# One encoder layer on one core: value loads a step ahead, w_out's maxima in the projections' sweep, its split by halves, MLP seam's loads regrouped

## Chip, core and metric

The kernel runs on one core of a Trainium2 chip as one program. The metric is the device time of one launch in microseconds (us); of several runs the median is given. Engines: PE multiplies matrices (PEld loads its weights), DVE, ACT and POOL work on vectors, SP issues nearly all of the transfers (DMA). PE writes to PSUM banks; everything else lies in SBUF tiles of 128 partitions.

## What is computed

One layer of a bidirectional encoder on x (2048 tokens, 1024 wide, float32):

```python
h = rmsnorm(x); proj = h @ w_in          # c_q | c_kv | k_rope | dq | dk | dv
# A: latent attention, 4 heads: q, k (128 + 64 rotary, normed), v from c_q, c_kv
o_mla  = softmax(q @ k.T * 192**-0.5) @ v
# B: differential attention, 4 heads of 2 maps, with a bias by distance
o_diff = (softmax(s1) - lam * softmax(s2)) @ dv     # each head RMS-normed
x = x + concat(o_mla, o_diff) @ w_out
x = x + relu(rmsnorm(x) @ w_up)**2 @ w_down
```

## The kernel before

Nearly every product is made from two float16 (or fp32r) halves of a float32 operand: `split` (L129 without a scale, L130 with one) writes the high half h on ACT and the low half l = x - h on DVE, and `mm3` (L134 to L136) multiplies hh, hl and lh. A weight or value tile in float32 ("raw") is so loaded, scaled by a factor that comes from a maximum, and split before PE can use it. Tiles come from rotating pools: L (7 buffers), W (22), P (8), X4 (3) and N2 (6); a new tile waits until some buffer of its pool has been read to its end. A scheduler sets each engine's order from the program's order and a simulated timeline; chains of `ordered` instructions keep theirs, and `behind` sets a point ahead of which an instruction may not go.

**The stages.** *Projections' sweep*: sixteen iterations of about 26 us, one token tile each. `load_x` (L371, pool X4) loads x two tiles ahead, `make_xT` (L385) transposes it on PE, `sweepA_mid` writes the transposed low-rank projection cT (also X4), and queries, keys and values go to DRAM (qA, qB, kA, kB, kR, vD).

*Attention*: 64 steps, 4 heads x 16 query tiles. A step handles one query tile of one head, in both attentions: three softmaxes, 0 for the latent attention and 1 and 2 for the two maps of the differential one. Its order is written out in PROG as tokens: S scores on PE (L735), M maxima on DVE (L745, L750), N the shift nm of the exponentials (L755, L756), E exponentials on ACT (L762), diff (L805), hi (L813 on ACT for d = 1, L140 on POOL for d = 0) and lo (L819, POOL) the two halves of the probabilities, T their transposing transfer (L824, SP), pv the product with the values (L836 to L838), store (L842, then a transfer to oD). A mark ' means the step before, '' (written ") the one before that. `load0` and `load1` are where the program may do a piece of other work. In heads 0 to 2 load0 prepares the next head: in odd steps a transposing key load (L588), and in steps VQ = (2, 6, 10, 15) a load of a block of values (L601, 512 KB, pool P) with its split (L130) directly behind it in the program. In head 3 load0 is `wo_step`: steps 0 to 7 load a block of w_out (L884), steps 1 to 8 take the maximum of the block before (`wo_stat`, L900, DVE), step 8 has `wo_front` (L907 to L911 with L889), step 9 `wo_scale` (a matmul and a maximum across partitions, L895 to L897, and L913 to L917); from step 9 on the same blocks are loaded a second time, and each is split by the next step. The last two splits stand at the start of `out_proj`.

*out_proj and the seam*: x + mix @ w_out for the sixteen tiles, its RMS norm and transposes (`out_back`, L1085, L1088). `combine_rows` (L1056 ff.) forms seven combinations of token halves (a Strassen scheme of 7 products for 2 x 2 blocks) and `put` splits them (L129): for the first half of the columns (c = 0) into hT[0], for the second into DRAM as hcD, from where they are loaded again as hT[1]. `up_load` loads raw w_up, `up_stat` (L1168 ACT, L1171 DVE) and `up_scale` (L1178 to L1184) find its scale, `up_weights` splits it.

*MLP up*: 32 steps (p, c), a pair of column blocks of w_up by a half of the tokens. A step's seven products go to three banks X, Y, Z; the first is evicted by ACT (L1300) into the half u11 of a tile `ca` (pool X4), others into `cb` (pool P) and, at the end, u21 of `ca` (L1312, L1316, L1321, L1322 on DVE, L1306, L1309, L1327, L1328 on ACT). `up_rest` then combines ca and cb on POOL (L1350 to L1359), splits the results (L1346 ACT, L1347 DVE) and stores them to uD. *MLP down* follows and is not touched.

## Time and profile before

| | us |
|---|---|
| median of 3 runs | 2865.11 (2864.14 to 2866.52) |
| the profiled execution | 2862.0 |
| its span | 2860.2 |
| PE / DVE / ACT / POOL busy in it | 2686.4 / 2140.0 / 1735.5 / 1715.3 |
| projections' sweep until | about 455 |
| attention | 455 to 1405 |
| out_proj | 1405 to 1621 |
| MLP up | 1621 to 2250 |
| MLP down | 2250 to 2860 |

A timeline row reads: start, duration, engine, line, operation, tile written <- tiles read, shape, and in brackets how long the engine had idled and what ended it. A row of a group gives busy time, mean ns of one, idle time ahead and its releaser. A wait is put down to the event that came last. A row of a stretch ends with PE's granted clock (1.00 is full), the busy share of the DMA engines, and GB/s.

### The profile page before, as it was taken

How to read it: one execution, taken by the hardware profiler on the slowest of the kernel's cores; microseconds unless marked ns; L12 is line 12 of the kernel's file. 1: busy time of each engine (PE TensorE's matmuls, PEld its weight loads, DVE VectorE, ACT ScalarE, POOL GpSimd, SP SyncE). 2: the span in 40 equal slices, each digit the busy share in tenths (PEclk: the TensorE clock that was granted, in tenths of full speed). 3: DMA queues.
4: the chain of work that ended last, by engine and by line, in shares of the span. 5: the costliest groups of instructions: out<-in, count | busy, mean ns of one | idle time of the engine just before them, and what ended most of it. 6: DMA issues, size and time to landing. Idle time of an engine off the chain costs nothing. (4 is left out here: it accounts for less than half of the span.)

```text
span 2860.2 us, 47994 instructions
## 1 busy us (share of the span) xinstructions
PE 2686.4 (94%) x16904; PEld 1574.4 (55%) x16904; DVE 2140.0 (75%) x4292; ACT 1735.5 (61%) x3814; POOL 1715.3 (60%) x1404
## 2 busy tenths in 40 slices
PE   7999998999999999889899988999999899999999
PEld 6878885666656666556555434444444344444444
DVE  8767778999998999889868777777776655555543
ACT  6545556888888888778757656666666433333332
POOL 5434334888888888778724355444444755565544
PEclk9999999999999999999999999999999999999999
DMA  5445557998999999899844753444444643333334
GB/s 194 123 116 133 136 131 186 199 204 184 203 207 200 195 203 204 189 197 188 207 165 146 241 175 107 133 133 133 133 146 158 234 151 133 133 123 116 133 103 169
DMA packets 994514, 469.35 MB, mean 164 GB/s; under 512 B 776128, under 2 KB 943040, under 8 KB 994272
## 3 DMA queue, kind: packets, MB, share of 16 engines
q1 hardware_dynamic: 994272, 466.29, 62.7%
q8 instruction: 132, 2.16, 0.3%
q14 instruction: 110, 0.90, 0.1%
HBM read 168.39 MB, written 132.12 MB: 105 GB/s over the span
## 5 line engine op out<-in xcount | busy, mean ns | idle before, releaser
L762 ACT ACTIVATE P<-D,nm,one 128x512 f32<-128x512 f32 x768 | 587.2, 774 | 132.0 <-DVE nm L756 70.8
L735 PE MATMUL D<-W,X 128*128 128x512 f16 x2304 | 573.0, 384 | 61.6 <-ACT P L762 58.7
L819 POOL TENSOR_TENSOR L<-P,L 128x1024 f16<-128x1024 f32 x256 | 553.9, 2172 | 32.4 <-ACT L L813 21.8
L750 DVE TENSOR_REDUCE nmx<-D 128x1 f32<-128x512 f32 (+3 forms) x768 | 450.8, 619 | 38.3 <-PE D L735 32.1
L836 PE MATMUL O<-W,L 128*128 128x128 f16 x2048 | 363.0, 220 | 16.3 <-DMA L<-L 9.1
L1459 POOL TENSOR_TENSOR W<-W,N 128x512 f32<-128x512 f32 x192 | 242.6, 1273 | 222.6 <-DVE W L1457 220.0
L735 PEld LDWEIGHTS <-X 128*128 128x128 f16 x2304 | 214.2, 99 | 282.7 <-issue 94.3
L837 PE MATMUL O<-W,L 128*128 128x128 f16 x2048 | 362.8, 220 | 1.1 <-DVE W L130 1.1
L838 PE MATMUL O<-W,L 128*128 128x128 f16 x2048 | 363.0, 220 | 0.0
L1457 DVE SCALAR_TENSOR_TENSOR W<-D,dsc,W 128x512 f32<-128x512 f32 x224 | 166.3, 747 | 255.8 <-PE D L136 255.8
L134 PE MATMUL D<-W,W 128*128 128x512 f16 (+2 forms) x822 | 313.6, 382 | 24.1 <-ACT P L1309 11.4
L135 PE MATMUL D<-W,W 128*128 128x512 f16 (+2 forms) x822 | 313.3, 381 | 3.2 <-DVE W L130 3.2
L136 PE MATMUL D<-W,W 128*128 128x512 f16 (+2 forms) x822 | 312.9, 381 | 0.6 <-DVE W L130 0.5
L140 POOL TENSOR_SCALAR L<-P 128x1024 f16<-128x1024 f32 x128 | 223.1, 1743 | 138.7 <-ACT P L762 138.7
L134 PE MATMUL D<-L,W 128*128 128x512 f16 (+1 forms) x644 | 249.5, 387 | 18.0 <-ACT X L1300 12.1
L134 PE MATMUL D<-L,P 128*128 128x512 f16 x648 | 247.1, 381 | 14.5 <-ACT N L1453 14.2
L135 PE MATMUL D<-L,W 128*128 128x512 f16 (+1 forms) x644 | 247.4, 384 | 0.0
L136 PE MATMUL D<-L,W 128*128 128x512 f16 (+1 forms) x644 | 247.3, 384 | 0.0
L135 PE MATMUL D<-L,P 128*128 128x512 f16 x648 | 246.9, 381 | 0.0
L136 PE MATMUL D<-L,P 128*128 128x512 f16 x648 | 246.8, 381 | 0.0
L836 PEld LDWEIGHTS <-L 128*128 128x128 f16 x2048 | 201.2, 98 | 53.0 <-DMA L<-L 15.7
L837 PEld LDWEIGHTS <-L 128*128 128x128 f16 x2048 | 201.2, 98 | 46.2 <-issue 12.8
(421 smaller groups left out, 5729.5 us busy)
## 6 DMA issues: line engine op xcount, KB each, us to landing
P<-uD SPq DMA_DIRECT2D x124, 448.0 KB, 4.9
uD<-P SPq DMA_DIRECT2D x96, 512.0 KB, 3.2
P<-in_w_up_dram SPq DMA_DIRECT2D x34, 512.0 KB, 4.7
W<-in_w_down_dram SPq DMA_DIRECT2D x32, 512.0 KB, 4.1
X<-in_x_dram SPq DMA_DIRECT2D x17, 512.0 KB, 3.6
vD<-N SPq DMA_DIRECT2D x32, 256.0 KB, 2.6
qA<-N SPq DMA_DIRECT2D x32, 256.0 KB, 2.6
oD<-N SPq DMA_DIRECT2D x128, 64.0 KB, 2.6
```

Source lines behind the costliest of these rows:

```text
L134: mm(o, ah, bh, start=first, stop=False, skip_group_check=more),
L135: mm(o, ah, bl, start=False, stop=False, skip_group_check=more),
L136: mm(o, al, bh, start=False, stop=last, skip_group_check=more),
L140: return G.tensor_scalar(o, i, sc, 0.0, ALU.mult, ALU.add)
L735: ordered(mm(s, st, mv[:, kc], start=j == 0, stop=j == len(self.passes) - 1))
L750: ordered(V.tensor_reduce(self.nmx[:, self.n : self.n + 1], s[:, c0 * P : c1 * P], AX, ALU.max))
L762: last_exp[:] = [act(o, self.ch[c], AF.Exp, bias=self.nm, scale=self.sg, accum_out=self.sm[:, c : c + 1])]
L819: ordered(G.tensor_tensor(hl[:, 1], self.soft[d].p[hf], hl[:, 0], ALU.subtract))
L836: ordered(mm(od, hT_, v[:, 0], start=kb == 0, stop=False))
L837: ordered(mm(od, hT_, v[:, 1], start=False, stop=False))
L838: ordered(mm(od, lT_, v[:, 0], start=False, stop=kb == NT - 1))
L1459: G.tensor_tensor(x, x, part.pop((t, to)), ALU.add)
```

## The change

**A.** VQ becomes (2, 6, 10, 12). The raw values of a block are loaded in the step ahead (1, 5, 9, 11), into pool W instead of P; the split keeps its place in the program. **B.** The eight blocks of w_out for the maxima are loaded in iterations 4 to 11 of the projections' sweep (pool X4), and their maxima taken on DVE one iteration later. `wo_front` and `wo_scale` run in head 1, steps 7 and 8. In head 3 every block is loaded once, in the even steps; its split is two halves of 512 columns, in the program one in each of the next two steps. One split is left at the start of out_proj. **C.** hcD is laid out as seven tiles, one for each combination, and hT[1] comes in 14 transfers of 512 KB instead of 56 of 128 KB, ten in step 1 of MLP up and four in step 2. All three early loads of w_up go into pool W, the third no longer into X4.

```diff
@@ -244,7 +244,7 @@
...
-    hcD = [dram(f"hcD{i}", [P, 7, 2, 512], F16) for i in range(4)]
+    hcD = [dram(f"hcD{i}", [2, P, 4, 512], F16) for i in range(7)]
...
@@ -612,7 +612,16 @@
...
+    def raw_wo(k, tag="W"):
+        raw = sb(tag, [P, D])
+        behind(nc.sync.dma_start(raw, a["w_out"][0, k * P : (k + 1) * P, :]))
+        return raw
+
+    def wo_stat(k, raw):
+        behind(V.tensor_reduce(wmx[:, k : k + 1], raw, AX, ALU.max, apply_absolute_value=True))
+
+
+    raww, WO_T = {}, range(4, 4 + KD)
...
@@ -670,11 +679,15 @@
...
         split_group(0)
         y0 = sweepB_group(tt, 0, xT[t])
+        if t - 1 in WO_T:
+            wo_stat(t - 1 - WO_T[0], raww.pop(t - 1))
         m = sweepA_up(tt, *fr.pop(t), *m)
         xT[t + 1] = make_xT(xs[t + 1])
         split_group(1)
         y1 = sweepB_group(tt, 1, xT[t])
         lower(t + 1)
+        if t in WO_T:
+            raww[t] = raw_wo(t - WO_T[0], "X4")
...
@@ -879,11 +892,6 @@
     wo = []
     OS = 2.0 ** 9
 
-    def raw_wo(k):
-        raw = sb("W", [P, D])
-        behind(nc.sync.dma_start(raw, a["w_out"][0, k * P : (k + 1) * P, :]))
-        return raw
-
...
@@ -895,9 +903,6 @@
...
-    def wo_stat(k, raw):
-        behind(V.tensor_reduce(wmx[:, k : k + 1], raw, AX, ALU.max, apply_absolute_value=True))
...
@@ -915,26 +920,23 @@
...
-    def split_wo(k, raw):
-        w = sb("W", [P, 2, D], F16)
-        behind(*split(w[:, 0], w[:, 1], raw, wsc[:, k : k + 1]))
-        wo.append((w[:, 0], w[:, 1]))
-
-    raww = []
+    def split_wo(k, raw, hfs=(0, 1)):
+        if 0 in hfs:
+            w = sb("W", [P, 2, D], F16)
+            wo.append((w[:, 0], w[:, 1]))
+        c = slice(512 * hfs[0], 512 * hfs[-1] + 512)
+        h, l = wo[k]
+        behind(*split(h[:, c], l[:, c], raw[:, c], wsc[:, k : k + 1]))
 
     def wo_step(qt):
 
-        raw = raww.pop() if raww else None
-        if qt != KD:
-            raww.append(raw_wo(qt if qt < KD else qt - KD - 1))
-        if 0 < qt <= KD:
-            wo_stat(qt - 1, raw)
-        if qt == KD:
-            wo_front()
-        elif qt == KD + 1:
-            wo_scale()
-        elif qt > KD + 1:
-            split_wo(qt - KD - 2, raw)
+        k, hf = divmod(qt, 2)
+        if hf == 0:
+            raww[k] = raw_wo(k)
+        if k:
+            split_wo(k - 1, raww[k - 1], (hf,))
+            if hf:
+                raww.pop(k - 1)
 
     def loads(h):
 
@@ -945,7 +947,10 @@
                 behind(turn_in(t.unsqueeze(1), src))
             if qt in VQ:
                 i = VQ.index(qt)
-                split_v(i // 2, h, kv[i // 2, h], raw_v(i // 2, h, i % 2, "P"))
+                split_v(i // 2, h, kv[i // 2, h], raw)
+            if qt + 1 in VQ:
+                i = VQ.index(qt + 1)
+                raw = raw_v(i // 2, h, i % 2, "W")
             if qt == NT - 1:
                 load_band(h)
             yield
@@ -1096,7 +1101,7 @@
             else:
                 o = sb("N2", [P, 2, 512], F16)
                 split(o[:, 0], o[:, 1], x)
-                dma(hcD[tq][:, i].rearrange("p l c -> p (l c)"), o.rearrange("p l c -> p (l c)"))
+                dma(hcD[i][:, :, tq].rearrange("l p c -> p l c"), o)
 
...
@@ -1105,13 +1110,11 @@
     def out_proj():
         order = ORDER
...
-        last_wo = raww + [raw_wo(KD - 1)]
         front = out_front(ot.pop(0), True)
         mix = next(front)
         for j in range(2):
             out_mid(order[0], j, *mix, (0,))
-        for k, raw in enumerate(last_wo):
-            split_wo(KD - 2 + k, raw)
+        split_wo(KD - 1, raww.pop(KD - 1))
         yield
         next(front)
         ot[1] = out_scale(*out_load(order[1]))
@@ -1137,7 +1140,7 @@
                 behind_products.append(down_max(0))
             for p, j in enumerate((4, 7, 13)):
                 if i == j:
-                    up_load(p, "W" if p < 2 else "X4")
+                    up_load(p, "W")
                 if i == j + 1:
                     behind_products.append(up_stat(p))
                 if i == j + 3 and p < 2:
@@ -1223,7 +1226,7 @@
             rawd.pop(g)
 
     qnext = []
-    VQ = (2, 6, 10, 15)
+    VQ = (2, 6, 10, 12)
...
@@ -1238,6 +1241,8 @@
                 fetch[1] = lambda: qnext.append(load_q(0, *divmod(n // 4 + 1, 4)))
             if h == H - 1:
                 fetch[0] = lambda: wo_step(qt)
+            if h == 1 and qt in (7, 8):
+                fetch[1] = (wo_front, wo_scale)[qt - 7]
             if h == H - 1 and qt == NT - 1:
                 loaded = out_load(ORDER[0])
             cur = Step(h, qt, list(qs), [kv[d, h] for d in range(2)])
@@ -1487,11 +1492,12 @@
             drain(made[n])
         if n == 1:
             drain(made["tokens"])
-            for i in range(7):
+        if n in (1, 2):
+
+            for i in ((0, 3, 4, 1, 5), (2, 6))[n - 1]:
                 b = hT[1, i] = [sb("W", [P, 4, 512], F16) for _ in range(2)]
                 for l in range(2):
-                    for tq in range(4):
-                        dma(b[l][:, tq], hcD[tq][:, i, l])
+                    dma(b[l].rearrange("p t c -> p (t c)"), hcD[i][l].rearrange("p t c -> p (t c)"))
...
```

The orders around it, as the scheduler leaves them. First SP in head 1, where the second block of head 2's values is loaded (W or P <-vD), with the key transposes (<-kB), stores (oD) and probability transposes (L<-L) about it. Before:

```order
L588 DMA_TRANSPOSE W_9014<-kB 128x1x2048
L116 DMA oD_87<-N_1892_10201 128x128
L824 DMA_TRANSPOSE L_10199<-L_10169 128x16x128
L588 DMA_TRANSPOSE X_1913_10293<-qA 128x4x512
L824 DMA_TRANSPOSE L_10199<-L_10169 128x16x128
L824 DMA_TRANSPOSE L_10305<-L_10171 128x16x128
L116 DMA oD_86<-N_1899_10256 128x128
L824 DMA_TRANSPOSE L_10305<-L_10171 128x16x128
L601 DMA P_10398<-vD_80 128x8x128
L116 DMA oD_88<-N_1934_10435 128x128
```

After (L824 is L837 now, and W_9041 is the tile that was W_9014):

```order
L588 DMA_TRANSPOSE W_9041<-kB 128x1x2048
L601 DMA W_10196<-vD_80 128x8x128
L116 DMA oD_87<-N_1901_10230 128x128
L837 DMA_TRANSPOSE L_10228<-L_10198 128x16x128
L588 DMA_TRANSPOSE X_1922_10322<-qA 128x4x512
L837 DMA_TRANSPOSE L_10228<-L_10198 128x16x128
L837 DMA_TRANSPOSE L_10334<-L_10200 128x16x128
L116 DMA oD_86<-N_1908_10285 128x128
```

The value load has moved up from behind both pairs of probability transposes to directly behind the key transpose.

ACT with the split of the same block: L762 is an exponential, L813 hi of map 1, L842 a store's scaling. Before:

```order
L813 ACTIVATE L_10405<-P_10219 128x1024
L842 ACTIVATE N_1934_10435<-O_10316,r_1865_10035 128x128
L762 ACTIVATE P_10453,sm_1901_10260<-D_10297,nm_1925_10387,one 128x512
L762 ACTIVATE P_10453,sm_1901_10260<-D_10301,nm_1925_10387,one 128x512
L130 ACTIVATE W_10400<-P_10398,vsc 128x8x128
L762 ACTIVATE P_10459,sm_1901_10260<-D_10313,nm_1925_10387,one 128x512
L762 ACTIVATE P_10459,sm_1901_10260<-D_10350,nm_1925_10387,one 128x512
L813 ACTIVATE L_10405<-P_10225 128x1024
```

After (L775, L826, L855 are the same three):

```order
L775 ACTIVATE P_10254,sm_1870_10059<-D_10110,nm_1893_10184,one 128x512
L775 ACTIVATE P_10254,sm_1870_10059<-D_10147,nm_1893_10184,one 128x512
L826 ACTIVATE L_10200<-P_10024 128x1024
L130 ACTIVATE W_10427<-W_10196,vsc 128x8x128
L775 ACTIVATE P_10275,sm_1870_10059<-D_10162,nm_1905_10271,one 128x512
L775 ACTIVATE P_10275,sm_1870_10059<-D_10187,nm_1905_10271,one 128x512
L775 ACTIVATE P_10279,sm_1870_10059<-D_10191,nm_1905_10271,one 128x512
```

The split has left its place between the exponentials of softmax 1 in the next step and stands behind the step's second hi, ahead of the exponentials of softmax 2.

ACT in head 3, a split of a w_out block (the row with rb_b). Before, in one of the last six steps:

```order
L762 ACTIVATE P_18700,sm_3356_18591<-D_18613,nm_3373_18640,one 128x512
L762 ACTIVATE P_18700,sm_3356_18591<-D_18619,nm_3373_18640,one 128x512
L130 ACTIVATE W_18732<-W_18492,rb_b 128x1024
L813 ACTIVATE L_18737<-P_18550 128x1024
L842 ACTIVATE N_3390_18767<-O_18648,r_3319_18359 128x128
L762 ACTIVATE P_18784,sm_3357_18592<-D_18629,nm_3381_18719,one 128x512
```

After, in one of the even steps:

```order
L775 ACTIVATE P_18731,sm_3364_18622<-D_18644,nm_3381_18671,one 128x512
L775 ACTIVATE P_18731,sm_3364_18622<-D_18650,nm_3381_18671,one 128x512
L826 ACTIVATE L_18768<-P_18581 128x1024
L130 ACTIVATE W_18763<-W_18297,rb_b 128x512 x2
L855 ACTIVATE N_3398_18798<-O_18679,r_3329_18397 128x128
L775 ACTIVATE P_18815,sm_3365_18623<-D_18660,nm_3389_18750,one 128x512
```

Both halves stand together (x2), now behind hi, and the odd steps hold none.

DVE in MLP up, step 1: L1312 and L1316 add the products of the step, L1171 sums squares of w_up, L1347 takes low halves of step 0's results, L130 splits weights. Before:

```order
L1347 TENSOR_TENSOR P_22750<-X_4013_22474,P_22750 128x2x4x128
L1171 TENSOR_REDUCE N_4029_22623<-N_4030_22624 128x128
L889 COPY N_4062_22855<-dmt_22853 128x128
L1347 TENSOR_TENSOR N_4051_22768<-X_4013_22474,N_4051_22768 128x4x128
L1171 TENSOR_REDUCE N_4029_22623<-N_4057_22822 128x128
L130 SCALAR_TENSOR_TENSOR W_22773<-N_4056_22776,rb_b,W_22773 128x512
L130 SCALAR_TENSOR_TENSOR W_22774<-X_3961_22196,rb_b,W_22774 128x2x512
L130 SCALAR_TENSOR_TENSOR W_22773<-N_4056_22776,rb_b,W_22773 128x512
L130 SCALAR_TENSOR_TENSOR W_22775<-X_3960_22195,rb_b,W_22775 128x512
L1312 SCALAR_TENSOR_TENSOR X_4045_22696<-D_22470,X_4045_22696 128x512
L1316 SCALAR_TENSOR_TENSOR P_22697<-D_22469,P_22697 128x512
```

After (L1352 was L1347, L1174 L1171, L897 L889, L1317 and L1321 were L1312 and L1316):

```order
L1352 TENSOR_TENSOR P_22717<-X_4013_22491,P_22717 128x2x4x128
L130 SCALAR_TENSOR_TENSOR W_22739<-W_22212,rb_b,W_22739 128x2x512
L1317 SCALAR_TENSOR_TENSOR X_4041_22663<-D_22487,X_4041_22663 128x512
L1174 TENSOR_REDUCE N_4029_22640<-N_4030_22641 128x128
L897 COPY N_4062_22830<-dmt_22828 128x128
L1352 TENSOR_TENSOR N_4047_22735<-X_4013_22491,N_4047_22735 128x4x128
L1174 TENSOR_REDUCE N_4029_22640<-N_4053_22789 128x128
L1321 SCALAR_TENSOR_TENSOR P_22664<-D_22486,P_22664 128x512
L130 SCALAR_TENSOR_TENSOR W_22740<-N_4052_22743,rb_b,W_22740 128x512
```

The first addition (L1317) now stands ahead of the squares' sums, the second behind them but ahead of two weight splits.

ACT there: the eviction of step 1's first product (L1300, then L1305) and the splits of step 0's results (L1346, then L1351). Before:

```order
L1346 ACTIVATE P_22746<-P_22725 128x2x4x128
L1346 ACTIVATE P_22750<-X_4013_22474 128x2x4x128
L1346 ACTIVATE N_4051_22768<-X_4013_22474 128x4x128
L1168 ACTIVATE N_4057_22822<-P_22565 128x1024
L130 ACTIVATE W_22773<-N_4056_22776,rb_b 128x512
L1300 ACTIVATE X_4045_22696<-D_22469 128x512
L130 ACTIVATE W_22774<-X_3961_22196,rb_b 128x2x512
```

After:

```order
L129 ACTIVATE N_4027_22632<-P_22562 128x512
L1305 ACTIVATE X_4041_22663<-D_22486 128x512
L129 ACTIVATE N_4028_22636<-P_22447 128x512
L1171 ACTIVATE N_4030_22641<-P_22581 128x1024
L1185 ACTIVATE rb_b<-usc_22621 128x1
L1332 ACTIVATE X_4013_22491<-D_22483 128x512
L1333 ACTIVATE X_4013_22491<-X_4013_22491 128x512
L1351 ACTIVATE P_22696<-P_22492 128x2x4x128
```

The eviction writes X_4045 before and X_4041 after, and it has moved ahead of step 0's last product (L1332) and of all the splits of its results.

## Prediction

> **What bounds the kernel now.** The page comes first. It gives the span and each engine's busy time:
>
> ```profile
> span 2860.2 us, 47994 instructions
> PE 2686.4 (94%) x16904; PEld 1574.4 (55%) x16904; DVE 2140.0 (75%) x4292; ACT 1735.5 (61%) x3814; POOL 1715.3 (60%) x1404
> ```
>
> PE is busy for 2686.4 us, so nothing that leaves its matmuls alone can win more than 173.8 us. The change leaves them alone, so what it can win or lose is PE's idle time. The second view is the busy time by stretches of time (start:end, length, then PE, PEld, DVE, ACT and POOL busy with instruction counts). In order: the middle of the projections' sweep; four attention steps that load and split nothing; the remaining steps of heads 0 to 2 from step 2 on (46 of them); steps 0 to 9 and 10 to 15 of the last head; the seam into the MLP.
>
> ```profile
> 204.50:416.00 211.50, 211.50 (x1020) 182.18 (x1019) 154.39 (x474) 108.64 (x343) 85.44 (x184) 1.00 0.52 126
> 504.40:559.10 54.70, 53.80 (x531) 35.36 (x529) 51.83 (x127) 46.51 (x110) 49.11 (x29) 1.00 0.99 207
> 488.70:1153.80 665.10, 624.78 (x6073) 410.08 (x6072) 606.94 (x1424) 558.68 (x1300) 566.59 (x324) 0.99 0.99 200
> 1153.80:1314.60 160.80, 141.71 (x1325) 91.67 (x1323) 139.74 (x324) 120.34 (x285) 118.58 (x69) 0.96 0.86 183
> 1314.60:1405.30 90.70, 81.85 (x787) 52.88 (x785) 86.41 (x188) 76.78 (x180) 75.18 (x43) 1.00 0.92 206
> 1621.00:1660.60 39.60, 25.75 (x126) 12.48 (x126) 28.31 (x39) 25.83 (x52) 16.37 (x11) 0.89 0.91 292
> ```
>
> The sweep is bound by PE without a gap (211.50 of 211.50). An undisturbed attention step takes 54.70/4 = 13.68 us and PE fills it. Against that, heads 0 to 2 lose 665.1 - 46 x 13.68 = 35.8 us, the last head 160.8 - 136.8 = 24.0 in its first ten steps and 90.7 - 82.1 = 8.6 in its last six. In the seam PE idles 13.9 of 39.6 us. Those four sums are what the change is aimed at. The third view, the waits by engine and releaser (total us, times, longest), says whose they are; the first three rows are of heads 0 to 2, the last is of the last head:
>
> ```profile
> ACT P L762 <- DVE nm L756: 31.8, 50, 0.9
> ACT W L130 <- DMA P<-vD: 30.2, 11, 3.9
> PE O L836 <- DMA L<-L: 9.1, 13, 2.2
> ```
>
> ```profile
> ACT P L762 <- DVE nm L756: 36.1, 18, 6.8
> ```
>
> In heads 0 to 2 the wait for the shift nm (L756) is the step's own rhythm (31.8/46 = 0.69 each). The wait of ACT's value split for its load is not: 30.2 us in 11 of the 12 splits, 2.75 each, and the exponentials are queued behind it on ACT. In the last head the wait for nm takes 36.1 us where 16 x 0.69 = 11.0 would be usual. The extra 25.1 us agrees with the 24.0 lost in its first ten steps.
>
> **A, values a step ahead.** The split waits because its raw tile is issued in the same step. Now it is issued a step earlier by the program, but the order shows that the scheduler pulls the split ahead too: on ACT it stands right behind hi11 (the second L813 of a step) and ahead of the next four exponentials, in the step of the load, and on SP the load stands right behind the next head's key transpose (L588). So I time the load from there. Rows of the split, of the transfers (size, median us from issue to landing; the kB and oD rows are the two queued at 716.36 and 718.78), and three of the steps where this happens, with SP's and ACT's timelines (start, duration):
>
> ```profile
> L130 ACT ACTIVATE W<-P,vsc 128x1024 f16<-128x1024 f32 x12 | 13.8, 1148 | 30.2 <-DMA P<-vD 30.2
> ```
>
> ```profile
> P<-vD SPq DMA_DIRECT2D x12, 512.0 KB, 4.4
> ```
>
> ```profile
> oD<-N SPq DMA_DIRECT2D x2, 64.0 KB, 2.9
> W<-kB SPq DMA_TRANSPOSE x1, 5.1
> ```
>
> ```profile
> 540.74 1.84 SPq L588 DMA_TRANSPOSE W<-kB  x1
> ...
> 716.36 2.33 SPq L588 DMA_TRANSPOSE W<-kB  x1
> 718.78 0.56 SPq L116 DMA_DIRECT2D oD<-N  x1
> ...
> 1060.00 3.19 SPq L588 DMA_TRANSPOSE W<-kA  x1
> ```
>
> ```profile
> 545.84 1.05 ACT L813 ACTIVATE L<-P 128x1024 f16<-128x1024 f32 x1
> 547.60 0.78 ACT L762 ACTIVATE P<-D,nm,one 128x512 f32<-128x512 f32 x1 [0.70 <-DVE s L793]
> ...
> 719.87 1.06 ACT L813 ACTIVATE L<-P 128x1024 f16<-128x1024 f32 x1
> 721.88 0.78 ACT L762 ACTIVATE P<-D,nm,one 128x512 f32<-128x512 f32 x1 [0.96 <-DVE s L793]
> ...
> 1065.13 1.06 ACT L813 ACTIVATE L<-P 128x1024 f16<-128x1024 f32 x1
> ```
>
> The raw load is issued when the key's issue ends: 542.6, 718.7, 1063.2. At 4.4 us to landing it is there at 547.0, 723.1, 1067.6; hi11 ends at 546.9, 720.9, 1066.2. ACT would wait 0.1, 2.2 and 1.4, 1.2 us on average. The other reading is that a transfer issued behind the key cannot overtake it: the 64 KB store issued at 718.78 landed 2.9 later, at 721.7, just behind the key (716.36 + 5.1 = 721.5). Then the value load lands 0.2 + (4.4 - 2.9) = 1.7 us or more after the key, at 547.5, 723.2 and (bounded by its own 4.4) 1067.6: waits of 0.6, 2.3 and 1.4, 1.4 on average. To this comes the split itself, 1.15, less the 0.83 (mean of 0.70 and 0.96) that the next exponential waits there anyway: 0.3. A split then costs 1.5 to 1.7 us, twelve 18 to 20.4, against 35.8 now: -15.4 to -17.8. I take **-16**. The trace gives no price for the queue on the key's step itself: at worst the transposed probabilities there come 1.0 late in each of the nine steps with both (+9, about what the wait of L836, 9.1, is now); at best the splits hide wholly (-30.2).
>
> [...]
>
> **B, w_out.** In the last head eight maxima (L900) go from DVE, with the waits that ended in front of the exponentials, and the whole splits of six steps become two halves each. These rows are of the last head; the third, of the whole run, gives the price of a half:
>
> ```profile
> L900 DVE TENSOR_REDUCE rb_b<-W 128x1 f32<-128x1024 f32 x8 | 9.7, 1216 | 10.5 <-DMA W<-in_w_out_dram 10.5
> L130 ACT ACTIVATE W<-W,rb_b 128x1024 f16<-128x1024 f32 x6 | 6.9, 1152 | 0.0
> ...
> L908 DVE TENSOR_TENSOR rb_b<-rb_b 128x8 f32<-128x8 f32 x1 | 1.7, 1708 | 0.0
> ...
> L895 PE MATMUL D<-ident,N 128*128 128x128 f32 x2 | 0.5, 326 | 1.1 <-ACT P L762 1.1
> ```
>
> ```profile
> L130 ACT ACTIVATE W<-N,rb_b 128x512 f16<-128x512 f32 x40 | 28.5, 711 | 7.2 <-POOL N L1199 7.0
> ```
>
> The maxima take 9.7 us busy and 10.5 waiting; all 24.0 of the first ten steps go. A step with a whole split costs 8.6/6 = 1.43 now. The order shows both halves back to back in the even steps 2 to 14, seven pairs, each longer on ACT by 2 x 0.711 - 1.152 = 0.27. I charge half of that: 7 x 1.57 = 11.0. The last head falls by 24.0 + 8.6 - 11.0 = **-21.5** rounded. If the halves hide wholly it is -32.6; at twice the price -10.6. At the start of out_proj one split of 1.15 on ACT goes: **-1** (0 to -3).
>
> [...]
>
> The maxima now lie in the sweep, 8 x 1.216 = 9.7 us of DVE work, where DVE is busy 154.39 of 211.50: hidden if PE's inputs have slack. SP and PE for one of the x tiles that share the buffers:
>
> ```profile
> 219.36 0.34 SPq L371 DMA_DIRECT2D X<-in_x_dram  x1
> ```
>
> ```profile
> 245.05 1.03 PE L385 MATMUL D<-ident,X 128*128 128x128 f32 x8
> ```
>
> The tile is issued 25.7 us ahead of its use. The bounds are 0 and 8 x 0.75 = 6 (about half a maximum showing up each time); I take **+1.5**. The scale's front (L908) and its matmul (L895) move to head 1. There they cost what the last head's rows show, 1.7 on DVE and a PE gap of 1.1, 2.8 at most and 0.5 at least: **+1.5**.
>
> **C, seam.** PE, ACT and DVE there:
>
> ```profile
> 1660.66 0.58 PE L134 MATMUL D<-L,W 128*128 128x512 f16 x1 [11.27 <-ACT X L1300]
> ```
>
> ```profile
> 1657.94 0.63 ACT L1346 ACTIVATE N<-X 128x512 f16<-128x512 f32 x1 [3.85 <-POOL X L1359]
> ...
> 1660.03 0.57 ACT L1300 ACTIVATE X<-D 128x512 f32<-128x512 f32 x1
> ```
>
> ```profile
> 1656.41 1.89 DVE L1171 TENSOR_REDUCE N<-N 128x128 bf16<-128x1024 bf16 x1
> 1658.21 1.00 DVE L889 COPY N<-dmt 128x128 f32<-128x128 f32 x1
> 1659.13 0.68 DVE L1347 TENSOR_TENSOR N<-X,N 128x512 f16<-128x512 f32 x1
> 1659.74 1.90 DVE L1171 TENSOR_REDUCE N<-N 128x128 bf16<-128x1024 bf16 x1
> ...
> 1668.51 0.69 DVE L1312 SCALAR_TENSOR_TENSOR X<-D,X 128x512 f32<-128x512 f32 x1 [1.01 <-PE D L136]
> 1671.10 0.69 DVE L1316 SCALAR_TENSOR_TENSOR P<-D,P 128x512 f32<-128x512 f32 x1 [1.90 <-PE D L136]
> ```
>
> PE idles 11.27 us until ACT evicts step 1's first product (L1300). That eviction writes a tile whose buffer is step 0's, not read to its end until L1346 at 1657.94. With up_load(2) out of that pool it has its own buffer, and in the order it stands ahead of L1346. So the stall goes, and DVE is late next: with PE 11.27 earlier, L1316 would be due at 1659.8, but between it and L1312 (due 1668.51 - 11.27 = 1657.2, 0.69 long) the order puts the four pieces that now stand ahead of both, 1.89 + 1.00 + 0.68 + 1.90 = 5.5 us, until 1663.4: 3.6 late. What covers that is two products of PE in between. Covered wholly, C is -11.3, not at all -7.7: **-9.5**; if another wait of DVE or of the regrouped loads takes the place, down to 0. The 14 grouped loads replace 56 on SP off PE's path: nothing, unless they come too late for step 4.
>
> **Sum.** -16 - 21.5 - 1 + 1.5 + 1.5 - 9.5 = -45. The profiled execution took 2862.0 us (2860.2 of span and 1.8 around it): 2817.0. It was 3.1 below the median of the three runs, 2865.11, so **2820**.
>
> **The rivals.**
> *The value splits gain nothing*: the load shares its step with a key transpose, so the wait per split stays near 2.75. For it: 718.78's store, held behind the key. Against: even so only 1.4 of waiting came out. A = 0: 2836.
> *The value splits hide*: loads landing before hi11 ends, as at 540.74 (0.1 late). A = -30.2: 2806.
> *The seam's wait is taken over by DVE*: busy 28.31 of 39.6 us there, and its order hardly moves. C = 0: about 2830.
> *Slower*: the sweep's buffers. x, the transposed projection and now a w_out block rotate through three buffers, and PE has no gap to give. If x's load has to wait for the maximum and eats its 25.7 - 4 us of lead, each of eight iterations loses PE time. It decides from (45 + 5.7)/8 = 6.3 us an iteration; at 7 it gives +56: 2876. Against: the maximum stands in the first half of the next iteration, so about half of that lead is left.
> *The change does not do what it says*: the scheduler hoists the splits back to their loads in A and the halves to one step in B; if the same holds for every wait, no change, 2865.
>
> **How the numbers follow.** Forecast .50 (2810 to 2832 by the bounds of its terms), splits gain nothing .18, splits hide .15, DVE takes over .12, slower .03, no change .02. The range 2803 to 2843 takes in the first four with some of their own spread. A measurement here can tell about 0.2%, 5.7 us, from no change: faster .95, same .02, slower .03.
>
> **What would show it.** After: ACT's W L130 wait for vD between 10 and 20 us; no L900 in the last head and 18 to 25 us less in it; no 11 us gap of PE behind step 1's eviction (L1305 then); the sweep's PE still without a gap. Wrong would be a PE gap in the sweep, vD waits at 30, or a new wait on DVE in the seam of 5 us or more.

## The result and the profile after

The changed kernel takes 2849.47 us (2847.49 to 2851.1, 4 runs) against 2865.12 (4 runs of the kernel before beside it): a ratio of 0.994 (95% interval 0.9927 to 0.9954). It is faster, by 15.7 us, where 45 were forecast, and it lies outside the range. The page of its profile (the profiled execution took 2850.76):

```profile
span 2849.0 us, 47954 instructions
PE 2685.7 (94%) x16904; PEld 1572.8 (55%) x16904; DVE 2154.2 (76%) x4299; ACT 1737.0 (61%) x3821; POOL 1719.2 (60%) x1404
```

PE does the same 16904 matmuls in the same busy time. The span is 11.2 us shorter, 10.5 of it PE's idle time (173.8 before, 163.3 after), and the stages, cut at the same instructions of both traces (the first score matmul of a step, ACT's eviction of an up step's first product), say where:

| stage | before | after | difference | forecast |
|---|---|---|---|---|
| until the attention starts | 455.8 | 462.2 | +6.4 | +1.5 |
| attention, steps 0 and 1 | 32.9 | 36.5 | +3.6 | 0 |
| heads 0 to 2 from step 2 on | 665.1 | 662.5 | -2.6 | -14.5 |
| head 3 | 251.5 | 236.5 | -15.0 | -21.5 |
| out_proj, to the first eviction of MLP up | 222.8 | 218.6 | -4.2 | -1 |
| up step 0 | 32.0 | 15.5 | -16.5 | -9.5 with the next row |
| up steps 1 to 7 | 141.1 | 155.0 | +13.9 | |
| up steps 8 to 31, then MLP down | 1059.0 | 1062.2 | +3.2 | 0 |

The row of up steps 1 to 7 reaches from step 1's first eviction to step 8's (the expectations below call it steps 1 to 8). The last row is unchanged code: MLP down alone took 635.8 to 643.9 us in the kernels below, which share it, so its 3 us are spread, not effect. The other stages spread less among kernels that share them: head 3 236.3 to 239.8, up steps 1 to 7 151.9 to 155.2, heads 0 to 2 657.8 to 667.4, steps 0 and 1 35.6 to 36.6, the start of the attention 460.2 to 465.4. So the miss lies in heads 0 to 2 above all (11.9), then in the seam, which gave back most of what it won (6.9), the last head (6.5) and the sweep (4.9). In the rows by stretch of time, DVE is busy for 92% and 95% of the two attention stretches:

```profile
498.70:1161.20 662.50, 624.88 (x6076) 409.90 (x6075) 610.18 (x1426) 557.92 (x1301) 563.35 (x320) 0.99 0.99 198
1161.20:1397.70 236.50, 214.95 (x2107) 141.37 (x2105) 224.91 (x505) 198.68 (x471) 199.33 (x112) 1.00 0.91 190
```

Two of the kernels below, e11 and e7, leave the attention as the change made it. Their heads 0 to 2:

```profile
501.00:1158.80 657.80, 618.25 (x6075) 407.80 (x6074) 608.68 (x1426) 557.85 (x1301) 562.24 (x320) 1.00 0.99 200
494.50:1161.90 667.40, 628.20 (x6075) 411.68 (x6074) 614.92 (x1426) 558.13 (x1301) 561.78 (x320) 0.98 0.99 197
```

The same matmuls keep PE busy for 618.25 us at a granted clock of 1.00 and for 628.20 at 0.98, while PE's idle time (the length less PE's busy time) is 39.6 and 39.2, and 37.6 in the row of the changed kernel. So the length of this stage differs by 9.6 us between the two by the clock alone, and PE's idle time is the safer measure of what a change does there.

The waits of heads 0 to 2, to be laid beside those of before:

```profile
ACT P L775 <- DVE nm L769: 46.3, 61, 2.5
...
PE D L748 <- ACT P L775: 23.4, 24, 3.3
ACT W L130 <- DMA W<-vD: 14.9, 10, 2.7
...
PE O L849 <- DMA L<-L: 8.1, 13, 1.5
```

A row of before that the prediction does not show:

```profile
PE D L735 <- ACT P L762: 27.1, 37, 3.5
```

ACT's wait for the value load came out as forecast: 14.9 us in ten waits, 1.2 for each of the twelve splits. It is half of the 30.2 of before, yet the stage hardly moved: the wait for the shift nm grew from 31.8 to 46.3, and PE's wait for the exponentials, which stand behind the split on ACT, fell by 3.7 only.

Of the signs that the prediction named, the vD wait of 10 to 20 us, the missing maxima of the last head and the missing gap of 11 us behind step 1's eviction are there. The last head is 15.0 us shorter, not 18 to 25. Two signs of an error are there too: the sweep's PE has a gap, and PE's wait for weight splits of DVE in MLP up's steps 0 to 7 is 7.3 us in all (0.5 before), where a new one of 5 was named.

### The profile page after: what moved, and what is told of

It reads as the page before. It is cut to its first block, busy times and chain, and to the rows that moved or that the text cites. A ratio compares the mean times of both kernels' runs of the same rounds, so it can differ in the third digit from the quotient of the medians.

```text
span 2849.0 us, 47954 instructions
## 1 busy us (share of the span) xinstructions
PE 2685.7 (94%) x16904; PEld 1572.8 (55%) x16904; DVE 2154.2 (76%) x4299; ACT 1737.0 (61%) x3821; POOL 1719.2 (60%) x1404
## 5 line engine op out<-in xcount | busy, mean ns | idle before, releaser
L775 ACT ACTIVATE P<-D,nm,one 128x512 f32<-128x512 f32 x768 | 586.7, 774 | 129.6 <-DVE nm L769 63.3
L763 DVE TENSOR_REDUCE nmx<-D 128x1 f32<-128x512 f32 (+3 forms) x768 | 451.5, 619 | 36.6 <-PE D L748 30.2
L134 PE MATMUL D<-W,W 128*128 128x512 f16 (+2 forms) x822 | 314.0, 382 | 19.1 <-ACT P L1314 7.2
L134 PE MATMUL D<-L,P 128*128 128x512 f16 x648 | 247.2, 382 | 14.5 <-ACT N L1458 14.1
L850 PEld LDWEIGHTS <-L 128*128 128x128 f16 x2048 | 200.8, 98 | 48.0 <-issue 15.5
```

The costliest lines, as they stand in the source:

```text
L134: mm(o, ah, bh, start=first, stop=False, skip_group_check=more),
L763: ordered(V.tensor_reduce(self.nmx[:, self.n : self.n + 1], s[:, c0 * P : c1 * P], AX, ALU.max))
L775: last_exp[:] = [act(o, self.ch[c], AF.Exp, bias=self.nm, scale=self.sg, accum_out=self.sm[:, c : c + 1])]
L850: ordered(mm(od, hT_, v[:, 1], start=False, stop=False))
```

## Experiments

The stage that an experiment is about is read from its trace in the same cuts, the whole time from runs beside the kernel before, which took 2864.75 to 2866.58 there. The whole times not given below are 2838.96 us (e1), 2844.22 (e5), 2821.61 (e6), 2846.36 (e7), 2852.34 (e8), 2844.68 (e9) and 2835.15 (e11). e1, e8 and e11 leave out a part of the computation.

**What heads 0 to 2 wait for.** One of the split steps of the changed kernel, on ACT, DVE and PE:

```profile
788.49 1.15 ACT L130 ACTIVATE W<-W,vsc 128x1024 f16<-128x1024 f32 x1 [2.33 <-DMA W<-vD]
...
793.86 0.78 ACT L775 ACTIVATE P<-D,nm,one 128x512 f32<-128x512 f32 x1 [0.93 <-DVE nm L769]
```

```profile
789.67 2.45 DVE L130 SCALAR_TENSOR_TENSOR W<-W,vsc,W 128x1024 f16<-128x1024 f32 x1 [1.45 <-ACT W L130]
792.04 1.35 DVE L763 TENSOR_REDUCE nmx<-D 128x1 f32<-128x512 f32 x2
```

```profile
790.44 4.22 PE L748 MATMUL D<-W,X 128*128 128x512 f16 x11 [2.21 <-ACT P L775]
```

The high half waits 2.33 us, PE then idles 2.21 for the exponentials behind it, and on DVE the low half, 2.45 us that the prediction gave no price of its own, stands ahead of the last two maxima, so the next shift is late too. This suggested two theories: the low half's place and work, or the rest of the wait.

`e1_no_low`:

```diff
-        split(v[:, :, 0, :], v[:, :, 1, :], raw, vsc[...])
+        act(v[:, :, 0, :], raw, AF.Copy, scale=vsc[...])       # heads 1 to 3
...
-                ordered(mm(od, hT_, v[:, 1], start=False, stop=False))
+                ordered(mm(od, hT_, v[:, 0 if self.h else 1], start=False, stop=False))
```

> The changed kernel, with the low halves of the values of heads 1 to 3 left out (the product uses the high half in their place, with as many matmuls). Stage: heads 0 to 2 from step 2 on, 662.5 us in the changed kernel. Theory 1 (the split's low half on DVE, 1.86 us twelve times plus its wait, now stands between two maxima ahead of the shift nm and costs its whole time): the stage falls by 20 to 30 us. Theory 2 (what is left is ACT's wait for the load, 14.9 us): it falls by 0 to 5, since that wait is untouched.

Measured: 658.2 us, inside the spread of kernels that keep the low half (657.8 to 667.4); ACT's wait 15.6. The first theory falls as the main cause: while something else holds the step, taking the low half away wins little. PE idles 35.3 us (658.2 - 622.86), 2 to 4 less than the 37.6 to 39.6 of the kernels that keep it.

`e2_load_earlier` and `e3_low_elsewhere` (the list VQ stays (2, 6, 10, 12)):

```diff
-            if qt + 1 in VQ:
+            if qt + 2 in VQ:
                 ... raw_v(i // 2, h, i % 2, "W")
-    ... M01 T01' ...   hi11' E20 ...
+    ... M01 load3 T01' ...   hi11' load2 E20 ...       # e2: load2 high half, load3 low half
+    ... sums1' load3 M10 ...   hi11' load2 E20 ...     # e3
```

> The changed kernel, with the raw values loaded one more step ahead (steps 0, 4, 8, 10) and the two halves of the split pinned to where they stand in it: high on ACT behind hi11, low on DVE behind M01 of the next step. ACT's wait for the load should go to 0. Theory 1 (the low half's place and work on DVE): the stage of 662.5 us falls by 0 to 8. Theory 2 (the load's wait): it falls by 12 to 18.

> As the run with the load one more step ahead, but the low half on DVE stands behind the sums that follow N0 (ahead of M10) instead of between M01 and M02, so no longer ahead of N0. Theory 1a (the place of the low half costs): the stage falls by 10 to 20 us below the run with the old place. Theory 1b (DVE is full, so only the work counts, wherever it stands): within 4 us of it.

Measured: 648.3 and 641.0 us; whole times 2829.81 and 2824.88. The first is the 14 us of the second theory, by number. The second is 7 lower, between its two expectations; two later kernels with the same heads took 643.6 and 640.5, so the place of the low half is worth 5 to 8 us in twelve splits (by PE's idle time as much: 26.8 us in e2, 19.3 to 22.2 in the three). The groups of e2 and of e3 show how:

```profile
L953 DVE SCALAR_TENSOR_TENSOR W<-W,vsc,W 128x1024 f16<-128x1024 f32 x12 | 21.5, 1789 | 0.0
```

```profile
L953 DVE SCALAR_TENSOR_TENSOR W<-W,vsc,W 128x1024 f16<-128x1024 f32 x12 | 15.3, 1276 | 0.0
```

Between M01 and M02 the same instruction takes 1.79 us on average, behind the sums 1.28.

`e4_undo_a` (VQ, the pool and the step of the load as before):

> The changed kernel with part A undone (values loaded and split in steps 2, 6, 10, 15 as before; B and C stay). Theories 1 and 2 both say that A as it was made brought next to nothing: the stage goes back from 662.5 to about 665 us, the whole time up by 0 to 5 us. If A did bring the 16 us of the forecast and something else took them, the stage goes to 675 or more.

Measured: 662.0 us, 2849.44 in all (the changed kernel: 2849.47). Part A brought next to nothing, as both theories say. But ACT's wait for the load is 23.6 us there, so 8.7 us less of waiting in the changed kernel won nothing that can be measured, which the second theory alone can't explain. The next run put that to the test.

`e5_old_place` (split pinned to the old places in steps 2, 6, 10, 15, raw values loaded one step ahead):

```diff
-    VQ = (2, 6, 10, 12)
+    VQ = (2, 6, 10, 15)
...
-    ... E10 E11 S23 E12 pv1"3 M22 M23 E13 N2 ...
+    ... E10 E11 load2 S23 E12 pv1"3 M22 M23 load3 E13 N2 ...
```

> The changed kernel with the values split at the places of the kernel before (high half on ACT after E11, low half on DVE ahead of N2, steps 2, 6, 10, 15), the raw values loaded one step ahead, so that no load is waited for. Theory 1 (the new place, ahead of E20 and between M01 and M02, costs more than the old one, which ate what the shorter wait gave): heads 0 to 2 from step 2 on take 636 to 643 us, at least 5 less than the 648.3 of the new place without the wait. Theory 2 (the places are worth the same, only the wait counts): 646 to 651.

Measured: 658.7 us. Both expectations fail. ACT waits for no load any more, and still nothing is won. What is new in its waits is PE's for the transposed probabilities L<-L: 28.7 us, against 9.1 before and 4.4 in e2. In e5 the value load stands in steps 1, 5 and 9, directly behind the key transpose; in e2 it stands in steps 0, 4, 8 and 10, in which no key is loaded. So e5 changed two things at once and does not settle what the places are worth. Hence a third theory: these two transfers in one step. It is tested by moving e2 by one step and nothing else.

`e9_collide`:

```diff
-    VQ = (2, 6, 10, 12)        # e2: loads in steps 0, 4, 8, 10
+    VQ = (3, 7, 11, 13)        # loads in steps 1, 5, 9, 11, behind a key transpose
```

> As the run with the load one more step ahead, with one constant changed: the steps of the list become 3, 7, 11, 13, so the raw values are loaded in steps 1, 5, 9, 11, directly behind a key transpose, and everything of the split stands one step later at the same places; ACT waits for no load in either. Theory 3 (the value load and the key transpose in one step hold up the probability transposes, and that was what the other run gained by moving the load): heads 0 to 2 from step 2 on take 655 to 663 us and PE waits 15 us or more for L<-L. Theory 2 (ACT's wait for the load is what costs): 645 to 651, as with 648.3.

Measured: 664.6 us against 648.3, with the split at the same places and no wait of ACT for a load in either. PE's wait for the transposes in e9, then in e2:

```profile
PE O L849 <- DMA L<-L: 28.2, 23, 3.2
```

```profile
PE O L849 <- DMA L<-L: 4.4, 7, 1.1
```

SP's queue in one such step of e9, and PE:

```profile
717.98 2.72 SPq L588 DMA_TRANSPOSE W<-kB  x1
720.75 0.58 SPq L601 DMA_DIRECT2D W<-vD  x1
721.43 0.52 SPq L116 DMA_DIRECT2D oD<-N  x1
722.06 3.34 SPq L837 DMA_TRANSPOSE L<-L  x1
725.45 2.02 SPq L588 DMA_TRANSPOSE X<-qA  x1
727.56 5.74 SPq L837 DMA_TRANSPOSE L<-L  x2
```

```profile
733.78 0.23 PE L849 MATMUL O<-W,L 128*128 128x128 f16 x1 [2.70 <-DMA L<-L]
```

Key and value block stand in the queue ahead of the first probability transpose, the query ahead of the next two, and PE idles until one of these has landed. The rows of e2 and of e9 for the stage:

```profile
494.80:1143.10 648.30, 621.49 (x6075) 409.44 (x6074) 609.17 (x1427) 557.64 (x1302) 569.49 (x322) 1.00 1.02 203
494.50:1159.10 664.60, 625.57 (x6076) 410.47 (x6075) 605.35 (x1427) 557.62 (x1302) 562.30 (x322) 0.99 0.98 199
```

Of the 16.3 us 12.2 are PE's idle time (26.8 and 39.0), the rest is its clock. So the theory holds for this pair. It holds for three of the four loads only: of PE's 28.2 us, 24.0 fall into steps 2, 6 and 10 (0.0 in e2), and 0.8 into step 12, behind the load of step 11, which stands beside a key as well. The queue shown has the query's transpose qA (L588) too; which of these transfers is needed for the wait stays open.

`e10_even_steps`, the changed kernel with one constant changed:

```diff
-    VQ = (2, 6, 10, 12)
+    VQ = (1, 5, 9, 11)
```

> The changed kernel with one constant changed: the list of steps becomes 1, 5, 9, 11, so the raw values are loaded in steps 0, 4, 8, 10, in which no key is transposed; the split is again pulled ahead to its load, and ACT waits for the load as in the changed kernel, some 10 to 15 us in all. Theory 3 (collision with the key): the stage falls from 662.5 to 645 to 652. Theory 2 (the wait): it stays at 657 to 665.

Measured: 649.7 us, 12.8 less than the changed kernel, and 2841.07 in all:

```profile
498.30:1148.00 649.70, 618.24 (x6074) 408.54 (x6074) 609.30 (x1426) 557.72 (x1301) 565.94 (x322) 1.00 1.03 203
```

PE's busy time, and with it the clock, makes 6.6 of the 12.8; PE's idle time falls from 37.6 to 31.5. The stage fell as the third theory says; but the expectation was wrong on ACT's wait, which is 0. The split is not pulled ahead to its load here: it starts 12.4 to 13.9 us, about a step, after the load's issue (4.2 to 6.6 in the changed kernel), and the load lands after 4.0 to 5.1 (4.2 to 6.2). So this run takes away the wait and the key together and does not tell the two theories apart. The pair of e2 and e9 does, but in kernels in which ACT waits for no load. The kernels side by side, in heads 0 to 2 from step 2 on (us):

| | stage | PE idle | ACT waits for values | PE waits for exponentials | PE waits for transposes |
|---|---|---|---|---|---|
| before: wait, no key | 665.1 | 40.3 | 30.2 | 27.1 | 9.1 |
| e4: wait, no key | 662.0 | 40.1 | 23.6 | 24.2 | 9.7 |
| changed kernel: wait and key | 662.5 | 37.6 | 14.9 | 23.4 | 8.1 |
| e5: no wait, key at three of four loads | 658.7 | 37.1 | 0 | 6.7 | 28.7 |
| e9: no wait, key | 664.6 | 39.0 | 0 | 4.5 | 28.2 |
| e10: neither | 649.7 | 31.5 | 0 | 10.9 | 2.8 |
| e2: neither | 648.3 | 26.8 | 0 | 8.4 | 4.4 |
| e3: neither, low half elsewhere | 641.0 | 20.8 | 0 | 6.5 | 6.5 |

With the wait, with the key beside the load, or with both, PE idles 37 to 40 us; only without either does it fall. In the changed kernel PE waits for the exponentials, which stand behind the split on ACT: 21.6 of the 23.4 us are in steps 2, 6, 10 and 12. It does not wait longer for the transposes than before. In e5 and e9, where the exponentials are not held up, it waits for the transposes instead. What share the late transposes have in the changed kernel is open, since no run has its shorter wait without the key.

**The last head.** In the changed kernel both halves of a w_out block go to one step. DVE and ACT there:

```profile
1201.62 3.58 DVE L130 SCALAR_TENSOR_TENSOR W<-W,rb_b,W 128x512 f16<-128x512 f32 x2
```

```profile
1207.79 0.78 ACT L775 ACTIVATE P<-D,nm,one 128x512 f32<-128x512 f32 x1 [4.10 <-DVE s L806]
```

Two low halves, 3.58 us, stand in the maxima of softmax 2, and the exponentials wait 4.10 us behind them.

`e6_wo_halves` (on top of e3; in the last head load2 is the high half of 512 columns, load3 the low half of the step before):

```diff
-        if k:
-            split_wo(k - 1, raww[k - 1], (hf,))
...
+                fetch[2] = lambda: wo_high(qt)      # qt >= 2, pinned behind hi11'
+                fetch[3] = wo_low                   # qt >= 3, pinned behind sums1'
```

> The kernel with the values' low half elsewhere, and in the last head the halves of w_out pinned one to a step, as the program meant them: high behind hi11, low on DVE behind the sums that follow N0 of the next step. Head 3 took 236.5 us in the changed kernel, 237.4 in the kernel this one is made from. Theory 1 (both halves in one step, with low halves ahead of the maxima of softmax 2, make the even steps and their neighbours long): head 3 falls to 224 to 230. Theory 2 (the work of the halves counts, wherever it stands): 233 to 238.

Measured: head 3 takes 227.9 us, 8.6 below the changed kernel:

```profile
1140.50:1368.40 227.90, 217.33 (x2107) 141.70 (x2105) 216.97 (x502) 197.71 (x467) 199.98 (x113) 1.00 0.99 198
```

DVE is still 95% busy (216.97), with 8 us less work in it, and PE fills 95%; PE's idle time falls from 21.5 to 10.6. The low halves alone, in the changed kernel and then here (the fourteenth stands behind the stage here):

```profile
L130 DVE SCALAR_TENSOR_TENSOR W<-W,rb_b,W 128x512 f16<-128x512 f32 x14 | 21.8, 1565 | 0.0
```

```profile
L947 DVE SCALAR_TENSOR_TENSOR W<-W,rb_b,W 128x512 f16<-128x512 f32 x13 | 9.7, 743 | 0.0
```

So the place counts, and not the number of halves: they are as many in both kernels, and a high half takes 0.72 us on ACT in both.

**The sweep.** PE's gap in the changed kernel, SP's queue ahead of it, and ACT:

```profile
220.84 0.69 PE L134 MATMUL D<-W,X 128*128 128x384 f32 x1 [3.52 <-ACT X L129]
```

```profile
199.13 0.35 SPq L617 DMA_DIRECT2D X<-in_w_out_dram  x1
...
207.48 0.33 SPq L371 DMA_DIRECT2D X<-in_x_dram  x1
207.86 0.62 SPq L307 DMA_DIRECT2D qB<-faret  x1
208.52 3.54 SPq L307 DMA_DIRECT2D kB<-farkh  x1
212.72 3.51 SPq L116 DMA_DIRECT2D vD<-N  x1
```

```profile
218.04 0.94 ACT L130 ACTIVATE N<-W 128x512 f16<-128x512 f32 x2 [1.99 <-DMA vD<-N]
```

The w_out block sits in the buffer that x needs. Before, x's load was issued right at the iteration's start (197.56); now it waits until 207.48, and what is queued behind it on SP, the far bias and the store of vD, is late with it. ACT waits for that store's buffer and evicts cT late, and PE waits for cT. x's load is late in each of the eight iterations with a block (10 to 17 us later than before), but a gap of this size comes only here.

`e7_sweep_w`:

```diff
-            raww[t] = raw_wo(t - WO_T[0], "X4")
+            raww[t] = raw_wo(t - WO_T[0], "W")
```

> The changed kernel with the eight blocks of w_out for the maxima in pool W instead of X4; the maxima stay. Theory 1 (a block takes the buffer that the next x tile needs; x's load then waits at the head of SP's queue, and stores behind it come late): the attention starts at 456 to 458 us instead of 462.2, and no gap of PE over 3 us is left at 220 us. Theory 2 (the maxima on DVE cost it): it still starts at 460 to 463.

Measured: the attention starts at 457.9 (458.5 in e12), and the gap at 220 us is gone. All maxima are still in it, so they cost at most the 2.1 us that are left against 455.8. By PE's idle time until the attention starts nearly nothing is left: 24.0 us before, 28.5 in the changed kernel, 24.5 here.

**The seam.** The 11.27 us stall is gone, and steps 1 to 7 take 13.9 us more. Those stretches before and after:

```profile
1660.00:1801.10 141.10, 129.43 (x586) 57.88 (x586) 102.39 (x104) 86.56 (x124) 78.65 (x51) 0.98 0.42 132
```

```profile
1631.80:1786.70 154.90, 136.44 (x607) 59.31 (x606) 118.32 (x118) 95.92 (x137) 89.61 (x57) 0.98 0.54 172
```

More instructions of every engine fall into them (118 instead of 104 on DVE, 607 instead of 586 on PE): work that was done ahead of the late eviction before, in up step 0:

```profile
1628.10:1660.00 31.90, 19.43 (x93) 9.22 (x93) 23.95 (x32) 19.45 (x37) 14.18 (x10) 0.88 0.91 295
1616.20:1631.80 15.60, 14.87 (x74) 7.32 (x74) 8.90 (x19) 10.04 (x25) 4.91 (x4) 1.00 0.77 258
```

So PE's busy time makes 7.0 of the 13.9, and its idle time 6.8 (11.7 and 18.5): much of what the two rows of the table exchange is only where the cut lies. Over up steps 0 to 7 together PE idles 24.2 us before and 19.1 after, 16.7 to 20.0 in the kernels that share them. Late weights are a part of what PE waits for, on DVE and PE:

```profile
1747.45 1.54 DVE L130 SCALAR_TENSOR_TENSOR W<-N,rb_b,W 128x512 f16<-128x512 f32 x1
1748.92 1.75 DVE L130 SCALAR_TENSOR_TENSOR W<-P,rb_b,W 128x512 f16<-128x512 f32 x1
```

```profile
1749.05 0.39 PE L136 MATMUL D<-W,W 128*128 128x512 f16 x1 [4.23 <-DVE W L130]
```

`e8_no_reload` leaves the loads of the second half out, `e11_no_weight_low` the low halves of the weights of steps 2 to 7:

```diff
-                b = hT[1, i] = [sb("W", [P, 4, 512], F16) for _ in range(2)]
-                for l in range(2):
-                    dma(...)
+                hT[1, i] = hT[0, i]                                      # e8
...
-        split(w[0][:, :, 0], w[0][:, :, 1], ra, c)
+        act(w[0][:, :, 0], ra, AF.Copy, scale=c)                         # e11, likewise the others
```

> The changed kernel with the second half of the columns (hT[1]) not loaded in the MLP's up stage: its products use the first half's tiles, so that part of the output is not computed; the 14 loads of 512 KB are gone. Steps 1 to 8 of the up stage took 141.1 us before and 155.0 in the changed kernel. Theory 1 (the 7 MB of loads in steps 1 and 2 hold up the stores and the loads of w_up, so its weights come late; before they ran in the stall of 11 us): steps 1 to 8 fall to 142 to 148. Theory 2 (making a fresh set of weights in each of these steps bounds them on DVE and ACT): 152 to 156.

> The changed kernel with the low halves of the up weights of steps 2 to 7 left out (the high half is used twice, with as many matmuls): six pieces of DVE work a step less, nothing else. Steps 1 to 8 of the up stage take 155.0 us in the changed kernel (151.9 to 155.2 in the kernels that share it), 149.0 without the second half's loads. Theory 2 (making the weights on DVE and ACT in each of these steps bounds them): they fall to 136 to 145. Theory 1 (the loads hold up the queue): 150 to 155.

Measured: steps 1 to 7 take 149.0 us without the loads and 142.2 without the low halves (kernels that share the stage: 151.9 to 155.2). e8 lies between its two theories: the loads cost some 3 to 6 us (by PE's idle time, 15.1 against 16.0 to 19.3, 1 to 4). PE no longer waits for late weights there (7.3 us in the changed kernel), but longer for evictions of ACT (12.6 instead of 6.4). e11 falls into the range of the second: with DVE's work down, its stretch is

```profile
1632.30:1774.50 142.20, 131.74 (x606) 58.86 (x605) 77.69 (x88) 95.47 (x137) 76.94 (x57) 1.00 0.58 187
```

and 40.6 us less of DVE (118.32 to 77.69) bring 12.7 us, 8.0 of them PE's idle time (18.5 to 10.5), the rest its clock (0.98 to 1.00). Every one of the first eight steps takes a fresh set of weights, and DVE's part of making it is the largest cost of the stretch that a run shows.

**All that helped.** `e12_all` is e3, e6 and e7 together, and the second half's loads spread over three steps:

```diff
-        if n in (1, 2):
-            for i in ((0, 3, 4, 1, 5), (2, 6))[n - 1]:
+        if n in (1, 2, 3):
+            for i in ((0, 3), (4, 1, 5), (2, 6))[n - 1]:
```

> All that helped, together: values loaded one more step ahead with the low half behind the sums that follow N0, one half of w_out to a step in the last head, the sweep's w_out blocks in pool W, and the second half's loads spread over steps 1 to 3 of the up stage (2, 3 and 2 pairs). If the stages add up: attention starts at 457 to 459, heads 0 to 2 take 640 to 645, head 3 226 to 230, steps 1 to 8 of the up stage 149 to 154; in all 2810 to 2820 us.

Measured: 2808.62 us (2805.92 to 2812.54), a ratio of 0.9799 to the kernel before (0.9784 to 0.9815), which beats both kernels. The attention starts at 458.5, heads 0 to 2 take 640.5, head 3 227.6, up steps 1 to 7 146.6. The last is better than expected; only the spread of the loads differs in that stage, and it is worth 5 to 9 us against the kernels that share the rest (3 to 6 by PE's idle time, 13.3 against 16.0 to 19.3). PE idles 126.4 us in the whole profiled execution, against 173.8 before and 163.3 in the changed kernel.

## Why the prediction was wrong

- **A, the failed step: the price of a split.** The wait was right (forecast 1.2 to 1.4 a split, measured 1.2). What failed is "To this comes the split itself, 1.15, less the 0.83 (mean of 0.70 and 0.96) that the next exponential waits there anyway: 0.3", and with it "twelve 18 to 20.4, against 35.8 now": all of the 35.8 was booked on the splits, and beyond the wait only 12 x 0.3 = 3.6 was to stay. In these terms 662.5 - 46 x 13.68 = 33.2 stayed. Taking away the wait and the key beside the load (e2) wins 14.2 of it, about the wait that was forecast; the other 19.0 are what the prediction priced at 3.6. Of these, the low half's place on DVE, which had no term, is worth 5 to 8 (e3), and at least 11 stay in every kernel here (11.7 in e3, 11.2 in e12); what they belong to is open. On PE the same shows directly: ACT's wait was halved, and PE's wait for the exponentials behind it went from 27.1 to 23.4 only.
- **A, the key's step.** "The trace gives no price for the queue on the key's step itself" set this at 0, with +9 as the worst. Where no split waits for its load, it costs 16.3 us (12.2 of PE's idle time, e9 against e2), more than that worst case. The change moved the load from steps without a key into steps with one, so even a split that waits for nothing wins little there: PE then waits for the transposes (e5, e9). The rival "the value splits gain nothing" came true in its time (e4: no difference), for a reason other than the one it named: the wait did fall. In e9 the probability transposes are issued behind key and value block and come late (28.2 us of PE's wait, 4.4 in e2); the prediction had not looked at them.
- **B, last head: mechanism right, size off.** The maxima's waits went. The remainder was mis-sized: 11.0 was charged for the seven pairs of halves, but 236.5 - 16 x 13.68 = 17.6 stayed. The price was taken from whole splits between E03 and hi; the pairs stand among the maxima. Spread, the remainder is 227.9 - 218.9 = 9.0. Of the 15.0 us that were won, PE's idle time is 6.4 (27.9 to 21.5) and its busy time 8.6 (141.71 + 81.85 before, 214.95 after, at a granted clock of 0.97 and 1.00): the 24.0 that were booked as waiting held some clock too.
- **Sweep: +6.4 for +1.5.** The slower rival's mechanism is real, in smaller form: x's load does wait for w_out's buffer, and e7 gives 4.3 us back. PE does not wait for x itself; the stores queued behind its load on SP were late. The prediction weighed x's lead and not the queue.
- **C, seam: rival 3.** The stall went and even 16.5 us were won in up step 0, but "C = 0: about 2830" was nearer than the forecast: -2.6 is left. In the kernels that share both stages it is -2.4 to -5.7, by PE's idle time -4.2 to -7.5. The step that failed is "with PE 11.27 earlier": the following steps are held by DVE's work on their weights above all (e11), and by the regrouped loads (e8), so PE does not stay that much earlier. The prediction followed one DVE instruction, 3.6 us late, and not the rate of the next seven steps.
- out_proj, forecast -1, shows -4.2 here and -4.9 to -0.4 in the runs that share it; PE's idle time falls by 2.3 here (9.7 to 7.4), the rest is its busy time. No run was made for its cause, and it stays open. The 3.6 us of steps 0 and 1 (2.7 to 3.6 in the kernels with the same attention) go with the first value split, whose low half now ends in them (2.47 us from 494.03): in e1, which leaves it out, 0.6 is left. No run was made for this alone.

## What to carry to other kernels

A load that is issued earlier must be priced in the step that it moves into: list what else that step queues, and who needs what is queued behind. A shorter wait is a gain only if the next thing on the path is not late as well (here PE idled 37 to 40 us with either of two waits, and 21 to 32 with neither), so follow the price of a split on every engine that has a half of it, at the place that the order gives it. A stall in front of a stretch that is held by something other than the stalled engine may be cover, not time: look at the pace of the steps behind it before counting it as won. And before two stages are compared by their length, take PE's busy time off both: with the granted clock it moved by 10 us in 660 here, between kernels that are the same in the stage.

## What the runs showed of the hardware

The same low-half instruction (128 x 1024, float32 to float16, two inputs) took 1.28 us on DVE at one place of a step (e3) and 1.79 on average at another (e2). In e2 POOL works during the whole of eleven of the twelve, and these take 1.64 to 1.91 us; the twelfth has no POOL work beside it and takes 1.28. In e3 POOL works for 0.4 us at most beside each, and all take 1.27 to 1.28. The halves of w_out (128 x 512) show the same: 0.74 to 0.75 us each in e6, with POOL at work for at most 0.06 us of them, and 0.92 to 2.62 in the changed kernel, with POOL at work for most of each. Three values' low halves of the changed kernel take 1.28 to 1.32 with POOL at work all the time, so that alone is not enough, and no run takes POOL's work away: whether it is the cause is not shown. The 6.2 us that DVE is spared in e3 (21.5 to 15.3) are about what the place is worth there; whether the shorter instruction or its place in the chain won them was not separated.
